# A decoder trunk's side work shifted by half chunks: value-weight sums every third tick, index scores and memory heads one tick later

## The chip, the cores and the metric

The kernel runs on one core of a Trainium2 chip. The metric is the device time of one execution in microseconds (us). Before the change it is 1921.55 us, the median of three runs (1921.13 to 1921.88). A chip core has a matrix engine (TensorE, PE in the profile, with PEld for its weight loads), a vector engine (DVE), an activation engine (ACT), a general engine (GpSimd, POOL) and a sync engine (SP) that issues DMA transfers; DVE, ACT and POOL issue their own instructions in program order, each waiting for the data it reads and for the buffers it writes.

## The reference: two layers of a three-part attention trunk

The input `x` has 512 tokens of width 2048, and there are 256 memory tokens. Two layers are computed, each

```python
h = einsum('bsd,dn->bsn', x, w_in)                 # one projection, split by columns
y_fox = fox_attention(fq, fk, fv, cum_logf) * silu(fg)      # 6 heads, a bias from log-sigmoid forget logits
y_dsa = dsa_attention(rope(dq), rope(dk), dv, rope(iq), rope(ik), iw) * silu(dg)   # 6 heads
y_mem = memory_attention(mq, k_mem, v_mem) * silu(mg)       # 4 heads into the memory tokens
x = layer_norm(ALPHA * x + concat([y_fox, y_dsa, y_mem]) @ w_out)
```

The sparse heads (dsa) keep the 128 best keys of each query. The choice comes from an index score: for each of 16 index heads, `relu(q_idx . k_idx)` times a weight of the query, summed over the heads. The forgetting heads (fox) use a running sum over tokens of `log_sigmoid(f_logit + b_forget)`.

## The kernel before: a stream of weight chunks, with side work hung onto ticks

**The chunks.** All weights pass as chunks of 128 x 2048 float32, in one list that Python writes out in full (the order on every engine is the program's order; nothing reorders it). Each half of a chunk (128 x 1024, a *half chunk*) is loaded by SP into one of 7 `raw` buffers (`load_w`, L259), split into a high and a low part by ACT (`whi`, L218) and DVE (`wlo`, L219) three half chunks ahead of use, and multiplied. Float32 accuracy is made of three matmuls for each product (L225 high x high, L226, L227, the two crossed ones). Sums go into eight PSUM banks that are handed out in turn.

**The stages of a layer.** Key and value of the memory (`mv`, `mk`); the small columns (index key, index weights, forget logits: `small`); eight chunks of index queries (`iq`); then the *values*: 70 chunks of kind `vs` that compute values, gates and other columns for five pairs of column blocks by a seven-product scheme (`PRODUCTS`: P1, P7, Q6, Q4, P2 in a first round of five pairs, and Q5, Q3 in a second round); then the heads' query and key chunks (`fq`, `fk`, `dq`, `dk`), in whose shadow the attention heads run; and the output projection by the same scheme.

**Weight sums.** Some of the seven products multiply a *sum* of weight blocks. Some are made in SBUF: `grow_w` (L284) lets POOL start a DMA that adds a second block onto a `raw` tile in place, and `pair_w` adds on DVE. The others are made in DRAM: POOL starts a DMA that copies one block to a DRAM tile `sum` (L427) and later a second one that accumulates the other block onto it (L407); when the product comes up, SP loads `sum` like any chunk, once the accumulation has landed. In the values stage these are T3 (for P7, all five pairs) and, last of all, T1 of pair 0 (for Q5, two chunks, at the start of the second round). POOL also starts the stores of the values (`store_v`, L980) to DRAM.

**Ticks.** Side work is written as Python generators. `tick()` steps every active generator; it is called after the first half of each chunk and at its end. A generator's `yield n` lets it sit out until the n-th tick from there. Generators begun with `whole=True` sit out the half-chunk ticks in the stages `out` and `vs`. Those that matter here:

- `all_sums` runs the weight sums in a fixed order through `paced` (L430): in the values stage one sum DMA for every `steps` ticks, and there a tick is a whole chunk; the other stages have numbers of their own in the table at L437.
- `small_work` (L602) turns the forget logits into their log-sigmoid: an exponential on ACT, then 15 tiny DVE operations of 128 x 24 (L619 to L631), a transpose, a scan, a store.
- `index_parts` (L672) makes from each roped `iq` chunk two operands `iqs` (high part on ACT, low part on DVE, L679). `index_scores` (L683) does one index head for each tick: six matmuls `ix` (L693, L694) from `iqs`, three ReLU on ACT (`rel`), three multiply-adds on DVE (`acc`, L702 for head 0, L704 after). It begins at L1316 after the first `iq` chunk.
- `mem_head` (L522) does one memory head: queries turned and split, scores `sm`, maximum on DVE (L539, L541), exponential on ACT (L544); a tick later the reciprocal of the sums on DVE (L551) and the scaling of the four blocks `pm` on ACT (L554); a tick later the transposes `ptm` on PE (L562) and their split; a tick later the gate; a tick later the product `po`. Four such heads run in each layer, the first across the end of the values and three in the heads' chunks. Beside them `attend` (L733) does the other heads, and after each `dq` or `dk` chunk DVE does `rope` (L578 to L581) on its bank.

Of the kernel before, what the change touches and what calls it, by code (L numbers as in the profile page):

```python
# [177 lines left out]
def kernel(  # L178
# [248 lines left out]
                            nc.gpsimd.dma_start(sums[key], src)  # L427
                        yield

    def paced(gen, steps=4):  # L430

        n = 0
        for _ in gen:
            n += 1
            while now[1] == "kv":
                yield 1
            yield {"heads": 1, "out": 3, "index": 1 + n % 2}.get(now[1], steps)  # L437
# [84 lines left out]
    def mem_head(l, j):  # L522
        load_head(("mq", j), MEMQ, j)
        km = slot("kmem", F32R)
        nc.sync.dma_start(km.bitcast(F32), km_d[l][j])
        yield 3
        tp = turned(("mq", j), "qk")
        q = slot("qh", F32R), slot("ql", F32R)
        split(tp, *q)
        yield 1  # L530
        k2 = (km[:, 0:256], km[:, 256:512])
        ps = [bank("sm"), bank("sm")]
        for qb in range(4):
            product(ps[qb // 2][:, (qb % 2) * 256:(qb % 2 + 1) * 256],
                    tuple(a[:, qb * P:(qb + 1) * P] for a in q), k2, True, True)
        nm, sums, rec = small("nm", 4), small("sums", 4), small("rec", 4)
        pr = [slot("pm"), slot("pm")]
        for b in range(2):
            nc.vector.tensor_reduce(nm[:, 2 * b:2 * b + 2], ps[b].rearrange("p (a k) -> p a k", a=2),  # L539
                                    axis=AX.X, op=ALU.max, negate=True)  # L540
        nc.vector.tensor_scalar(nm, nm, SCALE, None, op0=ALU.mult)  # L541
        for qb in range(4):
            cols = slice((qb % 2) * 256, (qb % 2 + 1) * 256)
            nc.scalar.activation(pr[qb // 2][:, cols], ps[qb // 2][:, cols], AF.Exp,  # L544
                                 bias=nm[:, qb:qb + 1], scale=SCALE, accum_out=sums[:, qb:qb + 1])
        del km, k2, q
        vm = slot("vmem", F32R)
        nc.sync.dma_start(vm.bitcast(F32), vm_d[l][j])
        load_head(("mg", j), MEMQ + 1, j)
        yield 1  # L550
        nc.vector.reciprocal(rec, sums)  # L551
        for qb in range(4):
            cols = slice((qb % 2) * 256, (qb % 2 + 1) * 256)
            nc.scalar.activation(pr[qb // 2][:, cols], pr[qb // 2][:, cols], AF.Copy,  # L554
                                 scale=rec[:, qb:qb + 1])
        yield 1
        pt = []
        for m in range(2):
            tp = bank("ptm")
            for qb in range(4):  # L560
                c = (qb % 2) * 256 + m * P
                nc.tensor.transpose(tp[:, qb * P:(qb + 1) * P], pr[qb // 2][:, c:c + P], ident)  # L562
            hi, lo = slot("pth", F32R), slot("ptl", F32R)
            split(tp, hi, lo)
            pt.append((hi, lo))
        del pr
        yield 1
        gate(("m", j), turned(("mg", j), "gt"))
        yield 1
        po = bank("po")  # L570
        for m in range(2):
            c = 2 * m * HD
            product(po, (vm[:, c:c + HD], vm[:, c + HD:c + 2 * HD]), pt[m], m == 0, m == 1)
        heads_out(H_FOX + H_DSA + j, ("m", j), po)
# [27 lines left out]
    def small_work(l, sm):  # L602

        yield 1
        tp = bank("iwt")
        for qb in range(4):
            nc.tensor.transpose(tp[:, qb * P:(qb + 1) * P], sm[:, qb * P:(qb + 1) * P], ident)
        tq = tp.rearrange("p (a b) -> p a b", a=4)
        iw = small("iw", 64, bufs=2)
        nc.scalar.activation(iw.rearrange("p (a b) -> p a b", a=4), tq[:, :, 64:80], AF.Copy,  # L610
                             scale=IDX_HEADS ** -0.5)
        idx["w"] = iw
        w = 4 * H_FOX
        x, e, d, s, s2, q = (small(c, w, bufs=2) for c in ("lx", "le", "ld", "ls", "lt", "lq"))
        nc.vector.tensor_copy(x.rearrange("p (a b) -> p a b", a=4), tq[:, :, 96:96 + H_FOX])
        nc.vector.scalar_tensor_tensor(e, x, -1.0, x, op0=ALU.mult, op1=ALU.min)
        nc.scalar.activation(e, e, AF.Exp)
        yield 1
        nc.vector.tensor_scalar(d, e, 2.0, None, op0=ALU.add)  # L619
        nc.vector.reciprocal(d, d)  # L620

        nc.vector.tensor_tensor(s, e, d, op=ALU.mult)
        nc.vector.tensor_tensor(s2, s, s, op=ALU.mult)
        nc.vector.tensor_scalar(q, s2, 1.0 / 17, None, op0=ALU.mult)
        for n in (15, 13, 11, 9, 7, 5, 3):
            nc.vector.scalar_tensor_tensor(q, q, 1.0 / n, s2, op0=ALU.add, op1=ALU.mult)
            if n == 11:
                yield 1
        nc.vector.scalar_tensor_tensor(q, q, 1.0, s, op0=ALU.add, op1=ALU.mult)
        nc.vector.tensor_scalar(x, x, 0.0, None, op0=ALU.min)  # L630
        nc.vector.scalar_tensor_tensor(q, q, -2.0, x, op0=ALU.mult, op1=ALU.add)  # L631
        yield 2
        tp = bank("lft")
        for qb in range(4):
            nc.tensor.transpose(tp[:H_FOX, qb * P:(qb + 1) * P],
                                q[:, qb * H_FOX:(qb + 1) * H_FOX], ident)
        r = slice(0, H_FOX)
        ones, crow = slot("ones"), slot("crow")
        nc.gpsimd.memset(ones[r], 1.0)
        nc.vector.tensor_tensor_scan(crow[r], ones[r], tp[r], 0.0, op0=ALU.mult, op1=ALU.add)  # L640
        nc.gpsimd.dma_start(crow_d[l], crow[r])
        yield 3
        tp = bank("cqt")
        for qb in range(4):
            nc.tensor.transpose(tp[:, qb * H_FOX:(qb + 1) * H_FOX],
                                crow[r, qb * P:(qb + 1) * P], ident[r, r])
        cq = small("cq", w, bufs=2)
        nc.scalar.activation(cq, tp[:, :w], AF.Copy, scale=1 / SCALE)
        forget["cq"] = cq
# [517 lines left out]
    for i, (kind, l, j, col, _) in enumerate(chunks):  # L1167
# [104 lines left out]
        if kind == "mk":  # L1272
            t = slot("kmem", F32R)
            split(ps[:, :256], t[:, 0:256], t[:, 256:512])
            begin(keep((km_d[l][j], t)), 1)
            if j == 3:
                load_index_tables()
        elif kind == "mv" and col == 3:
            for m in range(2):
                hi, lo = slot("vh", F32R), slot("vl", F32R)  # L1280
                split(out_ps[m], hi, lo)
                for part, t in enumerate((hi, lo)):
                    keep_values(l, m, part, t)
        elif kind in ("fq", "fk"):
            hi, lo = slot("qh", F32R), slot("ql", F32R)
            split(ps, hi, lo)
            (ks if kind == "fk" else qs)[kind[0], j] = (hi, lo)
        elif kind in ("dq", "dk"):
            t = rope(ps, cos_d, sin_d, HALVES, P, "rope")
            hi, lo = slot("qh", F32R), slot("ql", F32R)  # L1290
            split(t, hi, lo)
            (ks if kind == "dk" else qs)["d", j] = (hi, lo)
        elif kind == "vs":
            if col == 1:
                val_out(name, pair, zs)
                if name in VAL_ENDS:
                    del chains[VAL_CHAIN[name], pair], zs
        elif kind == "small":
            sm = slot("sm")
            nc.scalar.activation(sm, ps, AF.Copy)  # L1300
            r = slice(96, 96 + H_FOX)
            nc.scalar.activation(sm[r], ps[r], AF.Identity, bias=bfc[r, l:l + 1])
            t = index_rope(ps, 64, 0, nc.vector)
            kh2, kl2 = slot("kh2", F32R), slot("kl2", F32R)
            for r in (0, 64):
                nc.scalar.activation(kh2[r:r + 64], t[:64], AF.Copy)
                nc.vector.tensor_tensor(kl2[r:r + 64], t[:64], kh2.bitcast(F32)[:64],
                                        op=ALU.subtract)
            idx["k"] = (kh2, kl2)
            begin(small_work(l, sm))  # L1310
        elif kind == "iq":
            t = index_rope(ps, P, P, nc.gpsimd)

            begin(index_parts(j, t), 1)
            if j == 0:
                begin(index_scores(l), 2, last=True, whole=True)  # L1316
                begin(first_operands(), last=True)
            if j == 7:
                begin(val_operands(), 3, last=True)
            if j == 7:  # L1320
                index_tabs.clear()
# [147 lines left out]
```

## Time and profile before

| | |
|---|---|
| Median of three runs | 1921.55 us (1921.13 to 1921.88) |
| The profiled execution | 1921.65 us, of which the span from first to last instruction is 1919.9 us |
| Granted TensorE clock, mean | 0.996 of full speed |
| Busy: PE, DVE, ACT, POOL | 1891.7 us (99%), 1482.1 us (77%), 1019.6 us (53%), 364.5 us (19%) |
| DMA, mean rate over the span | 259 GB/s moved (page, part 2) |

PE is busy nearly all the time, so the rows to look for are those with PE's idle time and its releaser, written `[idle us <-releaser]` behind an instruction or as `PE tile line <- engine tile line: total us, times, longest us` in the view of waits. A tile's name in a row stands without its number. `PEclk` is the clock that TensorE was granted in a stretch, and a matmul's listed duration covers its passage through the array, so one follows another at a shorter distance than its duration.

### The profile page before, as it was taken

To read this page: it belongs to the slowest core of one execution; us is meant where nothing else is said; L and a number is where in the kernel's file an instruction comes from. 1 tells how busy PE (TensorE), PEld (TensorE's weight loads), DVE (VectorE), ACT (ScalarE), POOL (GpSimd) and SP (SyncE) were. 2 spreads that over 40 slices of the span, in tenths; PEclk is the share of its full clock that TensorE was granted. 3 is DMA by queue.
4 is the path that set the end of the run, shared out by engine and by line. 5 is a ranking of instruction groups with operands and counts; after the bars stand their busy time and mean duration, and the time that the engine had idled before them with its cause. 6 is when DMAs were issued, how large, how long until landed. Compare 5 with 4: busy or idle time off the path is not lost.

```text
span 1919.9 us, 26427 instructions
## 1 busy us (share of the span) xinstructions
PE 1891.7 (99%) x9250; PEld 1611.7 (84%) x9250; DVE 1482.1 (77%) x2395; ACT 1019.6 (53%) x1598; POOL 364.5 (19%) x603
## 2 busy tenths in 40 slices
PE   9999999999999999999999999999999999999997
PEld 8998888877888888888898988888888888888886
DVE  6889777879745677688897897889987457667898
ACT  5675444444455645555476764444545555555553
POOL 0122122111222011210061221111112121112101
PEclk9999999999999999999999999999999999999999
DMA  9877898889979689898888898887999787889965
GB/s 352 294 214 206 261 245 248 252 211 365 351 230 259 194 245 251 251 355 287 270 239 284 230 236 244 252 241 233 278 321 342 234 214 214 246 248 270 350 203 142
DMA packets 170610, 497.26 MB, mean 259 GB/s; under 512 B 17120, under 2 KB 62176, under 8 KB 162156
## 3 DMA queue, kind: packets, MB, share of 16 engines
q1 hardware_dynamic: 134604, 299.43, 45.3%
q0 software_dynamic: 35872, 196.13, 40.3%
q8 instruction: 73, 1.20, 0.2%
q14 instruction: 61, 0.50, 0.1%
HBM read 448.28 MB, written 166.75 MB: 320 GB/s over the span
## 4 chain that ended last, share of the span: by engine, by line
PE 82%; DVE 7%; ACT 5%; DMA 3%; issue 2%; POOL 0%; SPq 0%; DVEq 0%; ACTq 0%; POOLq 0%
PE v L227 13%; PE v L225 13%; PE v L226 13%; PE c L225 7%; PE c L227 7%; PE c L226 7%; PE z L226 4%; PE z L227 4%; PE z L225 4%; DVE wlo L219 2%; ACT whi L218 2%; DMA raw<-sum 1%; DMA raw<-in_wall_dram 1%; PE ix L693 1%; PE pt L777 1%
## 5 line engine op out<-in xcount | busy, mean ns | idle before, releaser
L219 DVE TENSOR_TENSOR wlo<-raw,whi 128x1024 fp32r<-128x1024 f32 (+1 forms) x521 | 637.7, 1228 | 238.3 <-ACT whi L218 236.0
L218 ACT ACTIVATE whi<-raw 128x1024 fp32r<-128x1024 f32 (+1 forms) x521 | 548.8, 1055 | 427.4 <-PE v L227 276.8
L225 PE MATMUL c<-xh,whi 128*128 128x512 f32 (+1 forms) x800 | 302.0, 377 | 2.9 <-DVE rope L580 2.9
L227 PE MATMUL c<-xh,wlo 128*128 128x512 f32 (+1 forms) x800 | 298.7, 373 | 0.0
L226 PE MATMUL c<-xl,whi 128*128 128x512 f32 (+1 forms) x800 | 298.0, 373 | 0.0
L225 PE MATMUL v<-whi,vxh 128*128 128x512 f32 x640 | 250.8, 392 | 2.8 <-ACT whi L218 1.8
L226 PE MATMUL v<-wlo,vxh 128*128 128x512 f32 x640 | 250.6, 392 | 0.8 <-DVE wlo L219 0.8
L227 PE MATMUL v<-whi,vxl 128*128 128x512 f32 x640 | 250.4, 391 | 0.0
L225 PE MATMUL v<-whi,xh 128*128 128x512 f32 x480 | 186.9, 389 | 0.0
L227 PE MATMUL v<-whi,xl 128*128 128x512 f32 x480 | 186.9, 389 | 0.0
L226 PE MATMUL v<-wlo,xh 128*128 128x512 f32 x480 | 186.9, 389 | 0.0
L226 PE MATMUL z<-wlo,yh 128*128 128x512 f32 (+1 forms) x434 | 168.4, 388 | 2.7 <-DVE wlo L219 2.6
L225 PEld LDWEIGHTS c<-xh,whi 128*128 128x128 f32 x800 | 150.4, 188 | 23.8 <-DVE rope L580 3.5
L225 PE MATMUL z<-whi,yh 128*128 128x512 f32 (+1 forms) x434 | 168.6, 388 | 0.0
L227 PEld LDWEIGHTS c<-xh,wlo 128*128 128x128 f32 x800 | 150.2, 188 | 21.8
L227 PE MATMUL z<-whi,yl 128*128 128x512 f32 (+1 forms) x434 | 168.0, 387 | 0.0
L226 PEld LDWEIGHTS c<-xl,whi 128*128 128x128 f32 x800 | 150.5, 188 | 20.6
L398 POOL TENSOR_TENSOR seen<-mark,mhalf 128x1 f32<-128x1 f32 x96 | 25.9, 270 | 651.9 <-DVE mark L397 614.3
L225 PEld LDWEIGHTS v<-whi,vxh 128*128 128x128 f32 x640 | 120.9, 189 | 28.6 <-ACT whi L218 2.2
L226 PEld LDWEIGHTS v<-wlo,vxh 128*128 128x128 f32 x640 | 120.9, 189 | 26.1 <-DVE wlo L219 1.1
L227 PEld LDWEIGHTS v<-whi,vxl 128*128 128x128 f32 x640 | 120.9, 189 | 25.3
L226 PEld LDWEIGHTS v<-wlo,xh 128*128 128x128 f32 x480 | 90.1, 188 | 18.8
(227 smaller groups left out, 3210.4 us busy)
## 6 DMA issues: line engine op xcount, KB each, us to landing
raw<-in_wall_dram SPq DMA_DIRECT2D x330, 512.0 KB, 7.7
sum<-in_wall_dram POOLq DMA_DIRECT2D x56, 1024.0 KB, 10.9
raw<-sum SPq DMA_DIRECT2D x112, 512.0 KB, 7.4
v<-vraw POOLq DMA_DIRECT2D x120, 256.0 KB, 6.9
raw<-in_wall_dram POOLq DMA_DIRECT2D x48, 512.0 KB, 8.0
vraw<-v SPq DMA_DIRECT2D x80, 256.0 KB, 5.9
other<-in_wall_dram SPq DMA_DIRECT2D x64, 256.0 KB, 9.3
x<-z POOLq DMA_DIRECT2D x28, 256.0 KB, 6.2
```

The costliest lines, as they stand in the source:

```text
L218: nc.scalar.activation(hi, src, AF.Copy)
L219: nc.vector.tensor_tensor(lo, src, hi.bitcast(F32), op=ALU.subtract)
L225: nc.tensor.matmul(ps, ah, bh, start=start, stop=False, skip_group_check=more)
L226: nc.tensor.matmul(ps, ah, bl, start=False, stop=False, skip_group_check=more)
L227: nc.tensor.matmul(ps, al, bh, start=False, stop=stop, skip_group_check=more)
L398: nc.gpsimd.tensor_tensor(seen, mark, mhalf, op=ALU.mult)
L693: nc.tensor.matmul(o, st[:, qb * P:(qb + 1) * P], kh2[:, :w], start=True, stop=False)
L777: nc.tensor.transpose(tp[tb][:, toff + (qb - kt) * P:toff + (qb - kt + 1) * P], pr[b][:, off + kt * P:off + (kt + 1) * P], ident)
```

## The change: four places where a step comes later or sooner

The values stage issues a sum DMA every third chunk and no longer every fourth. The index heads begin one tick (half a chunk) later. The small DVE operations of the forget logits wait a tick more after the exponential and are cut into four pieces by three yields, where one yield cut them in two. In each memory head the scaling L554, and all that follows it, comes one tick later; the reciprocal stays where it was, and so now comes a tick ahead of its use. Nothing is computed differently. Lines from L552 on have a number that is higher by one.

```diff
@@ paced, line 430: how many ticks the generator of the weight sums waits between two steps
-    def paced(gen, steps=4):
+    def paced(gen, steps=3):
@@ mem_head, line 549
         yield 1
         nc.vector.reciprocal(rec, sums)
+        yield 1
         for qb in range(4):
             cols = slice((qb % 2) * 256, (qb % 2 + 1) * 256)
             nc.scalar.activation(pr[qb // 2][:, cols], pr[qb // 2][:, cols], AF.Copy,
@@ small_work, line 617
         nc.scalar.activation(e, e, AF.Exp)
-        yield 1
+        yield 2
         nc.vector.tensor_scalar(d, e, 2.0, None, op0=ALU.add)
...
         for n in (15, 13, 11, 9, 7, 5, 3):
             nc.vector.scalar_tensor_tensor(q, q, 1.0 / n, s2, op0=ALU.add, op1=ALU.mult)
-            if n == 11:
+            if n in (13, 9, 5):
                 yield 1
@@ the main loop, line 1316
             if j == 0:
-                begin(index_scores(l), 2, last=True, whole=True)
+                begin(index_scores(l), 3, last=True, whole=True)
```

Three places in the order of instructions show it. The first is POOL at the end of the first round of the values in layer 0: `sum` are the DRAM sums (L407 the accumulating DMA), `raw<-in_wall_dram` the additions onto weight tiles (L284), `v` the stores of values. Before, around the first of the two last sums, T1 of pair 0:

```order
L284 DMA raw_3537<-in_wall_dram 128x1024
L284 DMA raw_3539<-in_wall_dram 128x1024
L407 DMA sum_3404<-in_wall_dram 128x2048
L284 DMA raw_3581<-in_wall_dram 128x1024
L284 DMA raw_3583<-in_wall_dram 128x1024
L980 DMA v_171<-vraw_3838 128x512
L980 DMA v_171<-vraw_3700 128x512
L980 DMA v_171<-vraw_3841 128x512
L980 DMA v_171<-vraw_3702 128x512
L980 DMA v_170<-vraw_3889 128x512
L980 DMA v_170<-vraw_3891 128x512
L407 DMA sum_3575<-in_wall_dram 128x2048
```

In the changed kernel the two last accumulations stand here:

```order
L284 DMA raw_3122<-in_wall_dram 128x1024
L284 DMA raw_3124<-in_wall_dram 128x1024
L284 DMA raw_3166<-in_wall_dram 128x1024
L284 DMA raw_3168<-in_wall_dram 128x1024
L407 DMA sum_3033<-in_wall_dram 128x2048
L407 DMA sum_3160<-in_wall_dram 128x2048
L981 DMA v_169<-vraw_3403 128x512
L981 DMA v_169<-vraw_3286 128x512
L981 DMA v_169<-vraw_3406 128x512
L981 DMA v_169<-vraw_3288 128x512
```

Both accumulations have moved ahead by one pair of column blocks and more: they now follow the four additions of pair 3 and stand ahead of the stores `v_169` of pair 3, where before they stood among and behind those of pair 4 (`v_171`, `v_170`). No sum stands behind them any more in this stage. `sum_3404` and `sum_3575` are renamed to `sum_3033` and `sum_3160`, since numbers follow the order of writing.

The second is DVE before the first index head in layer 0: `ld` to `lx` are the forget logits' operations, `iqs` the index operands, `wlo` the weight split, `vxl` an operand of the values. Before:

```order
L626 SCALAR_TENSOR_TENSOR lq_864<-lq_864,lt_863 128x24 x3
L397 COPY mark_913<-mhalf 128x1
L219 TENSOR_TENSOR wlo_928<-raw_822,whi_927 128x1024
L626 SCALAR_TENSOR_TENSOR lq_864<-lq_864,lt_863 128x24 x4
L629 SCALAR_TENSOR_TENSOR lq_864<-lq_864,ls_862 128x24
L630 TENSOR_SCALAR lx_859<-lx_859 128x24
L631 SCALAR_TENSOR_TENSOR lq_864<-lq_864,lx_859 128x24
L397 COPY mark_962<-mhalf 128x1
L679 TENSOR_TENSOR iqs_968<-rope_896,iqs_968 64x384
L679 TENSOR_TENSOR iqs_971<-rope_896,iqs_971 64x384
L873 TENSOR_TENSOR vxl_920<-vx_470,vxh_919 128x512
L219 TENSOR_TENSOR wlo_976<-raw_923,whi_975 128x1024
```

and now:

```order
L623 TENSOR_TENSOR ls_862<-le_860,ld_861 128x24
L624 TENSOR_TENSOR lt_863<-ls_862 128x24
L625 TENSOR_SCALAR lq_864<-lt_863 128x24
L627 SCALAR_TENSOR_TENSOR lq_864<-lq_864,lt_863 128x24 x2
L397 COPY mark_954<-mhalf 128x1
L680 TENSOR_TENSOR iqs_960<-rope_896,iqs_960 64x384
L680 TENSOR_TENSOR iqs_963<-rope_896,iqs_963 64x384
L874 TENSOR_TENSOR vxl_912<-vx_470,vxh_911 128x512
L219 TENSOR_TENSOR wlo_968<-raw_915,whi_967 128x1024
L592 TENSOR_TENSOR rope_995<-c_914,tab_715 128x384
L593 TENSOR_TENSOR rope_996<-rope_996,tab_717 128x384
L627 SCALAR_TENSOR_TENSOR lq_864<-lq_864,lt_863 128x24 x2
```

Two of the seven L626 steps stand ahead of the first `iqs` since the last weight split, where before the last four with L629 to L631 did; the rest comes later. On PE, the 24 matmuls of one more half chunk of `iq` now stand ahead of the first `ix`.

The third is ACT in the heads' chunks of layer 0, around the last memory head: `pm` L544 is its exponential, L554 its scaling, `pth` L218 splits of turned probabilities (of `ptm` for a memory head, of `pt` for another head), `whi` the weight split, `tanh` a gate, `qh<-rope` the roped queries. Before:

```order
L544 ACTIVATE pm_6056,sums_6054<-sm_6039,nm_6053 128x256 x2
L544 ACTIVATE pm_6057,sums_6054<-sm_6040,nm_6053 128x256 x2
L218 ACTIVATE whi_6076<-raw_5858 128x1024
L496 ACTIVATE tanh_6115<-gt_6110 128x512
L554 ACTIVATE pm_6056<-pm_6056,rec_6055 128x256 x2
L554 ACTIVATE pm_6057<-pm_6057,rec_6055 128x256 x2
L218 ACTIVATE pth_6153<-pt_6140 128x512
L218 ACTIVATE pth_6157<-pt_6141 128x512
L218 ACTIVATE pthl_6161<-pt_6142 128x256
L218 ACTIVATE whi_6164<-raw_6072 128x1024
L218 ACTIVATE qh_6198<-rope_6192 128x512
```

and now (L555 is the scaling):

```order
L544 ACTIVATE pm_6039,sums_6036<-sm_6022,nm_6035 128x256 x2
L218 ACTIVATE whi_6058<-raw_5849 128x1024
L218 ACTIVATE pth_6097<-ptm_6092 128x512
L218 ACTIVATE pth_6106<-ptm_6101 128x512
L218 ACTIVATE pth_6141<-pt_6128 128x512
L218 ACTIVATE pth_6145<-pt_6129 128x512
L218 ACTIVATE pthl_6149<-pt_6130 128x256
L218 ACTIVATE whi_6152<-raw_6054 128x1024
L218 ACTIVATE qh_6186<-rope_6180 128x512
L496 ACTIVATE tanh_6204<-gt_6199 128x512
L555 ACTIVATE pm_6038<-pm_6038,rec_6037 128x256 x2
L555 ACTIVATE pm_6039<-pm_6039,rec_6037 128x256 x2
```

The scaling stood ahead of `pth<-pt` and the next `whi`; it now stands behind that `whi` and the `qh` of the next roped chunk. In its old place stand the two `pth<-ptm` of the memory head before, which was moved by a tick too.

## The prediction, as recorded before the change was run

> **What bounds the kernel now.** I read the page first, then PE's waits, then PE's own timeline at the waits, and last the chain of waits, to see what each hangs on.
>
> ```profile
> PE 1891.7 (99%) x9250; PEld 1611.7 (84%) x9250; DVE 1482.1 (77%) x2395; ACT 1019.6 (53%) x1598; POOL 364.5 (19%) x603
> ```
>
> PE is busy for all but about 28 us of the span (1919.9 - 1891.7). The change neither adds nor removes a matmul, so all it can win is idle time of PE, or a lowered clock. The view of waits says who ends PE's idle time:
>
> ```profile
> PE ix L693 <- DVE iqs L679: 3.8, 2, 2.6
> PE c L225 <- DVE rope L580: 2.9, 2, 1.5
> PE v L225 <- ACT whi L218: 2.2, 2, 1.8
> PE po L227 <- DVE vl L219: 0.9, 2, 0.5
> ```
>
> The two `ix` waits, one for each layer, are the first index head's. The two behind `rope` and the two `vl` are in the heads' chunks of each layer, where a memory head runs. The largest wait on `whi` lies in layer 0, at 430 us, with two others close behind it. Three stretches, from the windows view (us, then busy time by engine, the clock, the DMA share, GB/s):
>
> ```profile
> 150.00:180.00 30.00, 30.00 (x138) 25.05 (x137) 29.00 (x45) 19.20 (x29) 8.09 (x12) 1.00 0.88 210
> 425.00:446.00 21.00, 17.42 (x62) 13.34 (x61) 15.37 (x24) 9.20 (x11) 2.88 (x4) 0.84 0.93 350
> 300.00:330.00 30.00, 30.00 (x134) 24.84 (x133) 22.42 (x33) 13.84 (x15) 8.51 (x14) 1.00 1.00 293
> ```
>
> **Term 1, the last sums: 7.1 us.** On PE's timeline in layer 0:
>
> ```profile
> 428.10 0.39 PE L226 MATMUL v<-wlo,vxh 128*128 128x512 f32 x1
> 428.32 0.39 PE L227 MATMUL v<-whi,vxl 128*128 128x512 f32 x1
> 430.52 0.49 PE L225 MATMUL v<-whi,vxh 128*128 128x512 f32 x1 [1.80 <-ACT whi L218]
> 431.78 0.80 PE L226 MATMUL v<-wlo,vxh 128*128 128x512 f32 x1 [0.77 <-DVE wlo L219]
> ...
> 437.89 0.40 PE L225 MATMUL v<-whi,vxh 128*128 128x512 f32 x1
> ...
> 439.72 0.39 PE L227 MATMUL v<-whi,vxl 128*128 128x512 f32 x1
> 441.12 0.50 PE L225 MATMUL v<-whi,vxh 128*128 128x512 f32 x1 [1.01 <-ACT vraw L968]
> ```
>
> Undisturbed, one such matmul starts 0.225 us behind the last (428.10 to 428.32, 0.227 over many). From start to start, the three waits cost 2.20 - 0.23 = 1.97, 1.26 - 0.23 = 1.03 and 1.40 - 0.23 = 1.17 us. Between the second and 437.89 lie 14 steps in 6.11 us, where 14 x 0.227 = 3.18 us would do: 2.93 us lost to a halved clock (the window shows 0.84). Together 7.1 us. The chain says what is late:
>
> ```profile
> 414.33 11.01 DMA sum<-in_wall_dram
> 425.40 3.90 DMA raw<-sum
> ```
>
> The accumulation of the second T1 sum starts at 414.33 and lands at 425.4; only then may SP load it. SP and POOL show the whole jam:
>
> ```profile
> SPq L259 <- DMA sum<-in_wall_dram: 39.1, 2, 22.3
> SPq L259 <- DVE wlo L219: 539.9, 219, 12.2
> 384.86 0.33 SPq L259 DMA_DIRECT2D raw<-in_wall_dram  x1
> 407.64 18.56 SPq L259 DMA_DIRECT2D raw<-sum  x4
> 328.49 0.86 POOL L284 DMA_DIRECT2D raw<-in_wall_dram  x1 [2.35 <-DVE wlo L219]
> 395.22 1.20 POOL L407 DMA_DIRECT2D sum<-in_wall_dram  x1
> 353.32 1.86 POOL L980 DMA_DIRECT2D v<-vraw  x3 [22.61 <-DVE vraw L957]
> ```
>
> SP issues nothing from 384.86 to 407.64 and again nearly to 425.4, with all later loads queued behind. In the changed order both accumulations follow the fourth L284 of pair 3, which starts at 328.49, and stand ahead of the stores of pair 3, which start at 353.32. So they are issued in this time, and even if the second only starts at 353 and the two land one behind the other at 12 us each (the median of sums there is in the next fence), both are down by 377, ahead of SP's turn. The earlier L427 copies move ahead likewise. SP then issues its loads when a `raw` buffer comes free, the next bound, and PE's lead of some three half chunks holds, as in 150 to 180 above where PE is busy for 30.00 of 30 us. Layer 1's sums are nearly done when its values begin and its trace has no such wait (SP's row counts two, both here): nothing there. I take all 7.1; the low end of this term is 0 (another wait just as long), the high end 7.1.
>
> What the cover costs: the denser sums lie beside additions onto weight tiles, on one POOL queue. Of these, the first row is undisturbed (155 to 265 us), the second stands behind an accumulation at 396 to 400:
>
> ```profile
> raw<-in_wall_dram POOLq DMA_DIRECT2D x8, 512.0 KB, 6.8
> sum<-in_wall_dram POOLq DMA_DIRECT2D x3, 1024.0 KB, 12.2
> raw<-in_wall_dram POOLq DMA_DIRECT2D x2, 512.0 KB, 13.8
> ```
>
> So an accumulation ahead doubles an addition's landing time from 6.8 to 13.8 us, and PE did not wait then (no wait in its timeline until 428.3). In the new order this meeting comes in pair 2, once. I price it at nothing, since it is the meeting that the trace already shows without a wait.
>
> [...]
>
> **Term 2, the index heads: 4.1 us.** PE and DVE before the first `ix`, layer 0, and PE in layer 1:
>
> ```profile
> 81.28 0.33 PE L226 MATMUL c<-xl,whi 128*128 128x384 f32 x1
> 81.45 0.34 PE L227 MATMUL c<-xh,wlo 128*128 128x384 f32 x1
> 82.98 0.39 PE L693 MATMUL ix<-kh,iqs 128*128 128x256 f32 x1 [1.19 <-DVE iqs L679]
> 80.92 0.83 DVE L626 SCALAR_TENSOR_TENSOR lq<-lq,lt 128x24 f32<-128x24 f32 x4
> 82.37 1.14 DVE L679 TENSOR_TENSOR iqs<-rope,iqs 64x384 fp32r<-64x384 f32 x2
> 1039.89 0.36 PE L693 MATMUL ix<-kh,iqs 128*128 128x256 f32 x1 [2.60 <-DVE iqs L679]
> ```
>
> In layer 0 the gap is 1.53 - 0.17 (the step at this width, 81.28 to 81.45) = 1.36 us, 0.17 over the listed wait; in layer 1 by the same 2.77. DVE runs four tiny steps, then L629 to L631, and only then `iqs`. The half-chunk delay puts 24 matmuls x 0.173 = 4.2 us of PE work between, more than either gap, and `iqs` itself moves ahead of seven tiny operations. The next heads find their operands half a chunk older than before. Gain 4.1; low end 0.
>
> Its price: the 16 heads take one tick each, so with a start half a chunk later one more of them ends up in the values stage, four for three. A head in that stage is three multiply-adds on DVE, which is 29.00 of 30 us busy there:
>
> ```profile
> 155.84 1.67 DVE L704 SCALAR_TENSOR_TENSOR acc<-rel,iw,acc 128x256 f32<-128x256 f32 x3
> ```
>
> DVE has 1.00 us to spare there and gets 1.67 more to do: it falls 0.7 us further behind. It splits three half chunks ahead of PE, each 2.72 us of PE (12 x 0.227), so a lag of 0.7 us is hidden unless the lead is already used up; priced at nothing, at most 0.7 in each layer.
>
> **Term 3, the memory heads: 4.9 us.** In layer 0:
>
> ```profile
> 639.97 0.63 ACT L218 ACTIVATE qh<-rope 128x512 fp32r<-128x512 f32 x1 [0.72 <-DVE rope L581]
> 642.63 0.50 PE L225 MATMUL po<-pth,vh 128*128 128x512 f32 x1 [0.15 <-ACT vh L218]
> 643.84 0.50 PE L227 MATMUL po<-pth,vl 128*128 128x512 f32 x1 [0.47 <-DVE vl L219]
> 650.93 1.71 ACT L554 ACTIVATE pm<-pm,rec 128x256 f32<-128x256 f32 x4 [2.27 <-DVE rec L551]
> 656.35 0.33 PE L227 MATMUL s<-qh,ql 128*128 128x384 f32 x1
> 658.13 0.50 PE L225 MATMUL c<-xh,whi 128*128 128x512 f32 x1 [1.45 <-DVE rope L580]
> ```
>
> The last wait costs 1.78 - 0.17 = 1.61 us, the two before it 0.15 + 0.47 and about 0.17 each to refill: 0.96. So 2.57 in layer 0; layer 1's waits are as long by the totals (`rope` 2.9 for two, `vl` 0.9 for two), less the `vh` one: 2.3. Cause: ACT stands for 2.27 us until the reciprocal comes, then scales for 1.71 us, and the splits behind it hold up DVE's `rope`, whose bank PE wants back. With the tick between, the reciprocal is long done when L555 comes to its turn; ACT scales behind the next `qh`, and the two `pth<-ptm` that take its old place need about 1.3 us (two of the size of that `qh`, 0.63), not 2.27 + 1.71. That is up to 2.7 us earlier for `pth<-pt`, against 1.61 of wait. Also the banks are handed out in turn and a tick's shift puts another bank under that `c`, one that was free longer. Late next is `ptm`, which now waits for a scaling that is issued only half a chunk (5.4 us) ahead, behind `rope` and `qh`. That `qh` ends at 640.6 here; without 1.71 us of scaling ahead it would end at 638.9, the scaling behind it at 640.6, and `ptm`, which now stands right ahead of the `po` of 642.63, is due some 1 us before that `po`, at 641.6. So about 1 us is to spare. I take 4.9; the low end is 0, where as much waiting comes up at `ptm` or `po`.
>
> **The sum.** 7.1 + 4.1 + 4.9 = 16.1 us. Against the profiled execution's 1921.65, which lies 0.1 above the median: 1905.5 us.
>
> **The rivals.**
> 1. *The memory heads only move their wait* to `ptm` or `po`. For it: the narrow 1 us, and that ACT and DVE take turns there. Against: less ACT time ahead of the bank's release. Terms 1 and 2 stay: 1921.65 - 11.2 = 1910.4.
> 2. *DVE falls behind in the first values* by the additional index head: 0.7 us a layer by the spare time above, up to a whole head, 1.67. Then 1906.9 to 1908.8.
> 3. *The first index head still waits*, its place having moved with something DVE does at the later tick: 1909.6. Against: `iqs` comes before that tick on DVE.
> 4. *The jam at 425 stays*, held by the `raw` buffers and not by the sum: 1912.6. For it: SP's waits are mostly for buffers, 539.9 us behind `wlo`. Against: the chain names the sum. If only the slow clock stays, 1908.4.
> 5. *Slower: the denser sums hold up the additions of pairs 1 to 3 in layer 0.* An addition is used some 14 us after its issue at the earliest in the row of 13.8 us without a wait; PE's lead of three splits adds about 4. So it decides beyond about 18 us of landing time. With two sums ahead, 6.8 + 2 x 12.2 = 31 us, a wait of 13 us; in two pairs 26 us, less the 16.1: about 1931. Against: the order puts no two sums between the additions of one pair ahead of it, only in pair 3 behind them. [...]
> 6. *Nothing is gained*, the waits all reappear: 1921.6.
>
> **How the numbers follow.** Forecast 0.52; rival 1 0.16; rival 2 0.10; rival 3 0.05; rival 4 0.07; rival 5 0.05; rival 6 0.05. The likeliest time is 1905.5. The range goes down to 1903.0, 2.5 us for the other waits of PE (on `wlo`, on `whi`) that may move by chance, and up to 1913.0, past rivals 1 to 4; left out are 5 and 6, mixtures of 1 with 4, and a tenth of the forecast's own case, about 0.18. A measurement of this kernel tells about 0.2% from no change, 3.8 us. Faster than 1917.7 are the forecast and rivals 1 to 4: 0.90, less 0.01 for mixtures. Within: rival 6 and half of a milder 5, 0.07. Slower: 0.04.
>
> **What would show it.** Step 1: no wait of SP on `sum<-in_wall_dram` in the values of layer 0, PEclk 1.00 around 425 and PE busy throughout. Step 2: no row `ix <- iqs`, and PE still busy for all of 150 to 180. Step 3: no `c <- rope` and no `po <- vl`; ACT's rows of `pm` on `rec` (2.27 us here) gone; a new row on `ptm` would be rival 1. A wait of `whi` on `raw<-in_wall_dram` between 200 and 400 us would be rival 5.

## The result and the profile after

| | Before | Changed |
|---|---|---|
| Median of four runs | 1921.34 us (1918.55 to 1921.88) | 1904.21 us (1903.45 to 1905.99) |
| Ratio, with 95% interval | | 0.9915 (0.9901 to 0.993) |
| Profiled execution, its span | 1921.65 us, 1919.9 us | 1903.59 us, 1901.8 us |
| Granted clock, mean | 0.996 | 0.998 |

The forecast was 1905.5 us, in a range of 1903.0 to 1913.0. The time lies 1.3 us below it.

PE's waits in the changed kernel (the view of waits; total us, times, longest), all rows of it:

```profile
PE z L226 <- DVE wlo L219: 2.5, 4, 0.7
PE warm L368 <- POOL mhalf L370: 1.4, 1, 1.4
PE v L225 <- ACT memh L218: 0.6, 2, 0.3
PE s L225 <- DVE rec L551: 0.4, 2, 0.2
PE c L227 <- DVE wlo L219: 0.4, 1, 0.4
```

The rows on `iqs`, `rope`, `vl` and `vraw` and the row of `v` on `whi` are gone. One row is new and small: `s` on `rec`, 0.4 us in both layers together. Most of what is left lies at the start and in the output stages, which the change does not touch. The stretches that the prediction named (the windows view: us, busy time by engine, clock, DMA share, GB/s):

```profile
75.00:90.00 15.00, 15.00 (x89) 14.91 (x88) 13.24 (x31) 11.49 (x19) 5.62 (x8) 1.00 0.84 284
150.00:180.00 30.00, 30.00 (x139) 25.07 (x139) 28.90 (x45) 18.73 (x30) 9.05 (x11) 1.00 0.90 208
425.00:446.00 21.00, 21.00 (x94) 17.42 (x93) 18.86 (x26) 10.76 (x14) 3.51 (x4) 1.00 1.01 350
636.00:664.00 28.00, 28.00 (x148) 23.92 (x147) 20.59 (x42) 15.06 (x32) 2.71 (x6) 1.00 0.81 219
1586.00:1613.00 27.00, 27.00 (x145) 23.15 (x144) 20.05 (x42) 14.46 (x31) 3.23 (x7) 1.00 0.78 195
```

PE is busy throughout in all of them, at full clock. Between 425 and 446 us it starts 94 matmuls where it started 62; from 636 to 664 us 148 for 136, by the same row of the kernel before:

```profile
636.00:664.00 28.00, 25.92 (x136) 21.46 (x136) 21.05 (x40) 14.44 (x33) 2.34 (x6) 1.00 0.71 223
```

The span of the profiled execution is 18.1 us shorter, and the three places of the prediction held 16.1 of that. Of the remaining 2 us, 1.1 lie in the first 20 us (PE busy for 16.81 us of them before, 17.88 now), which the change does not reach; in the profiles of the kernels below it runs from 16.5 to 18.0 us, with no order by kernel. The rest is not settled.

The jam on the sums is gone as worked out, in POOL's and SP's own rows (the timeline):

```profile
326.52 0.86 POOL L284 DMA_DIRECT2D raw<-in_wall_dram  x1 [2.35 <-DVE wlo L219]
327.06 2.04 POOL L407 DMA_DIRECT2D sum<-in_wall_dram  x2
...
385.61 19.41 SPq L259 DMA_DIRECT2D raw<-sum  x4
410.08 9.26 SPq L259 DMA_DIRECT2D raw<-in_wall_dram  x5
```

Both accumulations are issued at 327 us, right behind the addition of 326.52. SP issues its first load of a T1 sum at 385.61, where it was 407.64, and no wait of SP on `sum<-in_wall_dram` is left in its view of waits: what spaces its loads now is mostly the release of `raw` buffers (46.3 us of waits on `wlo` from 360 to 440 us), as foreseen. The DMA view of two short stretches shows what the sums meet (median us from issue to landing last; 263 to 273 us, the additions of pair 2 with accumulations among them, then 327 to 329 us, the last two sums):

```profile
raw<-in_wall_dram POOLq DMA_DIRECT2D x4, 512.0 KB, 9.8
...
sum<-in_wall_dram POOLq DMA_DIRECT2D x2, 1024.0 KB, 14.0
```

The last two sums landed after 14.0 us in the median of the two, so both within some 28 us of 327: by 356 us at the latest, about 30 us before SP's turn, and the meeting in pair 2 brought no wait of PE.

### The profile page after: what moved, and what is told of

It reads as the page before. It is cut to its first block, busy times and chain, and to the rows that moved or that the text cites. A ratio compares the mean times of both kernels' runs of the same rounds, so it can differ in the third digit from the quotient of the medians.

```text
span 1901.8 us, 26417 instructions
## 1 busy us (share of the span) xinstructions
PE 1886.0 (99%) x9250; PEld 1610.0 (85%) x9250; DVE 1477.7 (78%) x2395; ACT 1018.7 (54%) x1598; POOL 371.4 (20%) x603
## 4 chain that ended last, share of the span: by engine, by line
PE 89%; DVE 5%; ACT 3%; issue 2%; DMA 1%; POOL 1%; SPq 0%; DVEq 0%; ACTq 0%; POOLq 0%
PE v L227 14%; PE v L225 14%; PE v L226 14%; PE c L227 9%; PE c L225 9%; PE c L226 9%; PE z L226 4%; PE z L227 4%; PE z L225 4%; PE pt L778 1%; DVE wlo L219 1%; PE ix L694 1%; PE ix L695 1%; PE po L227 1%; PE po L226 1%
## 5 line engine op out<-in xcount | busy, mean ns | idle before, releaser
L218 ACT ACTIVATE whi<-raw 128x1024 fp32r<-128x1024 f32 (+1 forms) x521 | 548.5, 1055 | 420.4 <-PE v L227 273.8
```

What stands on the lines that cost most here:

```text
L218: nc.scalar.activation(hi, src, AF.Copy)
```

## The experiments: each part alone, each part left out, and the limits

All kernels of the table were timed in four or more runs beside the kernel before. A saving "by the ratio" is (1 - ratio) x 1921.3 us, and a difference between two kernels the difference of their ratios times 1921.3; an interval of a ratio is about 2.5 us to either side, so a difference of two ratios is uncertain by some 3.5 us.

| Kernel | Median, us | Ratio to before (95%) |
|---|---|---|
| the change | 1904.21 | 0.9915 (0.9901 to 0.993) |
| sums alone | 1912.11 | 0.9958 (0.9946 to 0.9971) |
| index and logits alone | 1918.91 | 0.9992 (0.9983 to 1.0001) |
| memory heads alone | 1915.04 | 0.9972 (0.9961 to 0.9983) |
| change without the sums | 1912.71 | 0.995 (0.9937 to 0.9963) |
| change without index and logits | 1908.5 | 0.9934 (0.9922 to 0.9947) |
| change without the memory heads | 1909.89 | 0.994 (0.9927 to 0.9954) |
| change, index start set back | 1906.01 | 0.9921 (0.9909 to 0.9934) |
| change, logits set back | 1905.27 | 0.992 (0.9907 to 0.9932) |
| change, reciprocal late too | 1905.21 | 0.992 (0.9906 to 0.9934) |
| change, a sum every 2 chunks | 1905.11 | 0.991 (0.9896 to 0.9923) |
| change, a sum every chunk | 1915.46 | 0.9966 (0.9952 to 0.9979) |

### The three parts, alone and left out

The sums alone, on the kernel before:

```diff
-    def paced(gen, steps=4):
+    def paced(gen, steps=3):
```

> The kernel before with the sums every third chunk and nothing else. By the theory of the terms: the 7.1 us around 428 to 441 us go (or 7.2 to 4.2, where the kernel before runs without its slow clock), the waits on iqs (4.1) and in the memory heads (5) stay: about 1914.3 us. By the rival (the last wait is for raw buffers, the sum only comes last by chance) another wait of some us stands at 428: above 1917.

Measured: 8.1 us less by the ratio. No wait is left between 420 and 450 us, and the waits on `rope` and `vl` stand as before, those on `iqs` with 2.5 us in all for 3.8:

```profile
420.00:450.00 30.00, 30.00 (x134) 24.82 (x134) 26.74 (x38) 15.17 (x18) 4.60 (x6) 1.00 0.96 319
```

The other way round, the change with `steps=4`:

> The changed kernel with the sums every fourth chunk again, so the index and memory-head edits without the sums. By the prediction's term: 7.1 us more, 1911.3. By the measurement of the sums alone on the kernel before (9.1 us): 1913.3. The wait on the last two sums should stand again at 425 to 441 us; where the clock stays at 1.00 there, the wait on vraw at its end should be longer (2.6 us) than where it is halved (1.0 us), since a slow PE lets ACT catch up.

Measured: 6.7 us more by the ratio (8.5 by the medians), and the jam is back. The clock stayed at full until its last wait (PE's steps are 0.23 us ahead of it, 0.43 behind it), and that wait, on `vraw`, is 2.64 us, as expected for this case. The term of 7.1 us holds from both sides, and so does its cause: nothing but the distance of the sums differs.

The memory heads alone (the one `yield 1` behind the reciprocal added to the kernel before) and the change without it:

> The kernel before with the scaling of the memory heads a tick after the reciprocal. By the theory 4.9 to 5.4 us go in the heads' chunks of both layers: about 1916.3. By the rival that the waits only move: 1920 to 1921.5.

> The changed kernel with the scaling of the memory heads back beside the reciprocal. By the prediction's term: 4.9 us more, 1909.1, with the waits on rope, vl and vh in both layers as before. By the measurement of this edit alone (6.1 us): 1910.3.

Measured: 5.4 us less alone, 4.8 us more when left out, by the ratios. In the change without it PE's view of waits has the old rows back, and no others of their size in the heads' chunks:

```profile
PE c L225 <- DVE rope L580: 2.9, 2, 1.5
PE po L227 <- DVE vl L219: 0.9, 2, 0.5
```

The index heads with the logits alone (`begin(index_scores(l), 3, ...)`, `yield 2` behind the exponential, yields at 13, 9 and 5), and the change without these:

> The kernel before with the index heads a tick later and the logits' small operations in four pieces. By the theory: both gaps before the first ix go, 4.1 us, and the jam at 428 stays: about 1917.3. By the rival (the additional index head in the values makes DVE late) 1.4 to 3.4 us come back between 150 and 200 us and in the same place of layer 1: 1918.7 or more.

> The changed kernel without the two edits on the index and the logits: sums and memory heads alone. By the term of the prediction the two gaps of 1.4 and 2.8 us stand again: 1908.3. By the measurement of these two edits on the kernel before (2.3 us): 1906.5. If they do nothing for the time: 1904.2.

Left out of the change, they cost 3.7 us by the ratio (4.3 by the medians), near the term of 4.1; in the profile the waits on `iqs` that are back come to 2.5 us in all. Alone on the kernel before they save 1.5 us by the ratio, with an interval from 3.3 us saved to 0.2 us lost, which the 4.1 us lie outside of. Its profile has no wait on `iqs` and no new one between 150 and 200 us, so the rival that the additional head makes DVE late falls. What it has is a jam at 428 us of larger size than in the profile of before, and in that kernel the jam is still there to vary. Between these two profiles the jam's size makes 0.9 us of the difference (below). PE's waits on `z`, in the output stages, are 1.8 us longer in its profile as well; why is not settled.

### What of the index edits is needed

The index start back to 2 with the logits in four pieces; and the start at 3 with the logits as before:

> The changed kernel with the index heads' start set back a tick, the logits' operations still in four pieces. DVE then has some 0.8 us less ahead of the first iqs than in the kernel before (two tiny steps and L629 to L631). If the tick is what removes the wait: gaps of about 0.55 us (layer 0) and 1.95 us (layer 1) at the first ix stand again, 2.5 us in all, 1906.7. If the cut of the logits' operations does it alone: no gap, 1904.2.

> The changed kernel with the logits' operations in two pieces as before, the index heads still a tick late. If the tick removes the wait: no gap at the first ix in either layer, 1904.2. If the cut is needed too: a gap of 1 us or more in layer 1, 1905.5 or more.

With only the logits' edit of the two, a wait at the first `ix` remains in layer 0 (first row, PE's timeline); with neither edit it is that of before in layer 0 (second row) and 1.36 us in layer 1 (third row):

```profile
82.88 0.39 PE L694 MATMUL ix<-kh,iqs 128*128 128x256 f32 x1 [0.17 <-DVE iqs L680]
```

```profile
83.33 0.39 PE L694 MATMUL ix<-kh,iqs 128*128 128x256 f32 x1 [1.18 <-DVE iqs L680]
1028.87 0.36 PE L694 MATMUL ix<-kh,iqs 128*128 128x256 f32 x1 [1.36 <-DVE iqs L680]
```

With only the tick no row of `ix` on `iqs` is in the view at all. So either edit removes most of this wait: 0.5 us of it is left in both layers with the logits' cut alone (its row reads `0.5, 2, 0.4`), none with the tick alone. The times, 1906.0 and 1905.3 us, are not told apart from the change's by their intervals. The forecast of 2.5 us left for the cut alone was too high, in good part because it started from a layer-1 gap of 2.77 us that turned out to be one execution's. In another execution of the kernel before, the row was

```profile
1041.61 0.35 PE L693 MATMUL ix<-kh,iqs 128*128 128x256 f32 x1 [1.71 <-DVE iqs L679]
```

### Is it the early reciprocal or the late scaling?

In the prediction the memory heads' waits came from ACT, which stood up to 2.27 us for the reciprocal ahead of the scaling. To tell that from the mere shift of all later steps by a tick, the reciprocal was put a tick late too, directly ahead of the scaling:

```diff
-        yield 1
+        yield 2
         nc.vector.reciprocal(rec, sums)
-        yield 1
         for qb in range(4):
```

> The changed kernel with the reciprocal a tick later too, directly ahead of the scaling, so that everything behind it stays a tick late as in the changed kernel but ACT waits for the reciprocal again. If the late place of the scaling and of what follows (other PSUM banks, the scaling behind qh) is what removes PE's waits: none come back, 1904.2. If it is the early reciprocal: PE waits for rope, vh or vl or for ptm in both layers, up to the 5 us of before, 1906 to 1909.

ACT's group for the scaling (the lines view: busy us, mean ns, idle before and its releaser) in the kernel before, in the change, and in this kernel:

```profile
L554 ACT ACTIVATE pm<-pm,rec 128x256 f32<-128x256 f32 x32 | 13.7, 498 | 13.4 <-DVE rec L551 13.4
```

```profile
L555 ACT ACTIVATE pm<-pm,rec 128x256 f32<-128x256 f32 x32 | 13.6, 496 | 0.0
```

```profile
L554 ACT ACTIVATE pm<-pm,rec 128x256 f32<-128x256 f32 x32 | 13.7, 498 | 8.0 <-DVE rec L551 8.0
```

ACT's wait is back with 8.0 of 13.4 us; at the last memory head of layer 0 it is 1.08 us, where it was 2.27. PE's waits on `rope`, `vl` and `vh` are not back: none is among its rows, and the time is 1905.2 us, 1.0 above the change by either measure, inside the intervals. So in the late place PE's waits stay away though ACT stands for the reciprocal again, and the early reciprocal adds too little to be told from noise. A full wait of 2.27 us in the late place was not run.

How the late place helps can be read on DVE. In the kernel before, DVE stands for ACT's `pth` ahead of the `rope` that PE waits for (first row); in this kernel (second row) and in the change the same step has no wait, for the scaling no longer stands ahead of that `pth` on ACT:

```profile
653.15 1.29 DVE L219 TENSOR_TENSOR ptl<-pt,pth 128x512 fp32r<-128x512 f32 x2 [2.32 <-ACT pth L218]
```

```profile
641.51 1.28 DVE L219 TENSOR_TENSOR ptl<-pt,pth 128x512 fp32r<-128x512 f32 x2
```

This speaks for the order on ACT; what the other bank under the next `c` adds was not taken apart.

### How dense the sums may be

The change with the sums every second chunk, and at every chunk:

> The changed kernel with a sum every second chunk. If the distance of the sums only has to be short enough for the last two to be down before SP's turn: 1904.2, no PE wait between 150 and 450 us. If denser sums cost (rival 5, additions landing beyond 18 us): waits of whi on raw there and a time above 1906.

> The changed kernel with a sum at every chunk. The order has one accumulation between the additions of pairs 0 and 2 each, so by the trace so far additions of 12 to 14 us and no PE wait: 1904.2. By rival 5: two sums ahead of an addition, landing at 25 us or more, a wait of some 7 us or more in one or two pairs: 1911 to 1918.

Every second chunk is as good as every third, and no better: there was no more wait to remove. At every chunk the time is 9.8 us above the change by the ratios, within what rival 5 gave. PE's timeline and ACT's in this kernel:

```profile
225.68 0.50 PE L225 MATMUL v<-whi,vxh 128*128 128x512 f32 x1 [1.03 <-ACT whi L218]
226.94 0.79 PE L226 MATMUL v<-wlo,vxh 128*128 128x512 f32 x1 [0.76 <-DVE wlo L219]
246.00 0.49 PE L225 MATMUL v<-whi,vxh 128*128 128x512 f32 x1 [2.32 <-ACT whi L218]
...
224.57 1.06 ACT L218 ACTIVATE whi<-raw 128x1024 fp32r<-128x1024 f32 x1 [3.06 <-DMA raw<-sum]
244.89 1.06 ACT L218 ACTIVATE whi<-raw 128x1024 fp32r<-128x1024 f32 x1 [7.51 <-DMA raw<-in_wall_dram]
```

And the DMA view: POOL's issues from 200 to 245 us with a sum every chunk, and SP's from 190 to 245 us, in this kernel and then in the change:

```profile
sum<-in_wall_dram POOLq DMA_DIRECT2D x3, 1024.0 KB, 19.9
raw<-in_wall_dram POOLq DMA_DIRECT2D x4, 512.0 KB, 20.1
...
raw<-in_wall_dram SPq DMA_DIRECT2D x7, 512.0 KB, 12.6
raw<-sum SPq DMA_DIRECT2D x4, 512.0 KB, 15.7
```

```profile
raw<-in_wall_dram SPq DMA_DIRECT2D x8, 512.0 KB, 5.0
raw<-sum SPq DMA_DIRECT2D x4, 512.0 KB, 8.3
```

The additions onto weight tiles land after 20.1 us, and ACT, then PE at 246.00, waits for them (the addition issued at 224.34 us, the `whi` behind it at 244.89). With a sum every second chunk the additions of the same stretch took 11.5 us, and PE was busy for all of 190 to 250 us. This is the mechanism of rival 5 with its threshold between: no wait at 13.8 us, waits at 20.1.

The late landing is not all of it. That addition was also issued late, by POOL's timeline in this kernel:

```profile
216.47 0.88 POOL L284 DMA_DIRECT2D raw<-in_wall_dram  x1 [2.29 <-DVE wlo L219]
223.80 0.83 POOL L407 DMA_DIRECT2D sum<-in_wall_dram  x1 [6.46 <-DMA sum<-in_wall_dram]
224.34 1.20 POOL L284 DMA_DIRECT2D raw<-in_wall_dram  x1
```

POOL stands 6.46 us at an accumulation until a sum's DMA has landed, by the order the copy that it adds onto, and the addition behind it in POOL's order waits with it. From the second to the third addition of the pair it takes 7.9 us here and 2.7 in the change (211.80 to 214.52), where POOL has no such wait from 150 to 250 us; nor has it with a sum every second chunk. The copy and the accumulation of one sum are too close together when a sum DMA is issued for each chunk of 5.4 us and a sum lands after 19.9. How much of the 9.8 us is the late issue and how much the slow landing was not taken apart.

The PE wait at 225.68 is on one of SP's loads of a sum, on another queue. With the denser sums SP's loads of weights take 12.6 us here for 5.0 in the change, and its loads of sums 15.7 for 8.3, so the loads slow down with a queue that they do not stand in. How the DMA engines share their time between the queues is not shown.

### The kernel before once more

> The kernel before once more, for its clock at 425 to 446 us. Where the slow clock goes with the wait: clock 0.84 and 17.4 of 21 us busy there again, 1921.5. [...]

1924.82 us in its one run, and the clock was lowered there again (0.89 from 420 to 450 us). The time is 3.3 us above the one expected for that, and above all runs of this kernel beside it (1918.62 to 1923.25). Most of that lies in the first 20 us, where the clock was lowered too:

```profile
0.00:20.00 20.00, 16.86 (x59) 12.73 (x60) 9.81 (x13) 11.12 (x15) 0.74 (x7) 0.91 0.90 307
```

PE starts 59 matmuls there where it started 68 in the first execution, at clock 1.00: 9 x 0.227 = 2.0 us. An execution with clock 1.00 at the jam was not among the profiles of this kernel. What this and the other kernels that still have the jam show is put together below.

## Why the prediction was right, point by point

- **PE's idle time is all there is to win, in three places.** Right: the waits named are gone, no others of their size came, and the three parts, alone, save 8.1, 5.4 and 1.5 us, left out, cost 6.7, 4.8 and 3.7, where 7.1, 4.9 and 4.1 were reckoned. Either three add up to about 15 us, of the 16.3 that the change's own ratio gives. Each part is uncertain by 2 to 3.5 us, so that the sum of 16.1 came within 0.2 us of the measured saving is in part luck.
- **Term 1, the sums.** Right in mechanism and size: the accumulations are issued at 327 us, right behind the fourth addition of pair 3, at the early end of the stretch that the order gave (328 to 353 by the times of before). They land some 30 us before SP needs them, and SP now stands for buffers, without a wait of PE. Wrong in the split of its 7.1 us: 2.93 us were charged to the lowered clock. A run of the jam at full clock (the last section) shows that a part of it would have been waiting instead.
- **Its cover, priced at nothing.** Right: additions among accumulations in pair 2 landed after 9.8 us (median of four) without a wait of PE.
- **Term 2, the index heads.** The tick covers the wait in both layers, as worked out, and the additional head in the values costs nothing: PE is busy for 30.00 of 30 us from 150 to 180. The size was one execution's for layer 1 (2.77 us; the wait was 2.60 there, and 1.71 in another execution). Four other profiles with the old start and the logits as before list 2.5 to 2.9 us for both layers where this one listed 3.8; with 0.17 us for each gap that makes 2.8 to 3.2, so 4.1 us was about 1 us too much.
- **Term 3, the memory heads.** Right in size (4.8 to 5.4 for 4.9), and `ptm` has no wait, so the spare time of about 1 us sufficed. Of the causes that it named, the reciprocal's wait on ACT proved the lesser. With 8.0 of its 13.4 us back, PE waits for `rope` or `vl` no more than in the change. The place of the scaling behind the next `qh` carries the gain; the share of the other banks, also named, is not known.
- **The rivals.** Rivals 1 to 4 did not come: no `ptm` or `po` wait, no lateness of DVE, no `ix` wait, no wait of PE for want of `raw` buffers at 425. Rival 5 was real, but its point of decision lies between a sum every second chunk and one every chunk, and a part of it is POOL's own standing for a copy, which the prediction did not name.

## What to carry to other kernels

Where one queue issues work for others in a fixed order, read the chain back from the late load to the instruction that started it, and issue that instruction earlier, where its queue has time to spare. It can be too dense: a sum DMA for each 5.4 us chunk was too many here, where sums then landed after 19.9 us and an accumulation stood for its own copy. An engine's own idle time (ACT's 13.4 us on the reciprocal) is no measure of what its removal gives; ask which instruction of the bounding engine waits, and test the shift without the cure. A gap read in one execution can be that execution's: the largest of the index gaps was 0.9 us shorter in the next.

## What the runs showed of the hardware

The cost of the lowered clock was not what its rows suggest. The jam at 420 to 450 us (windows view) in the kernel before, in its second execution, with the memory heads alone, with index and logits alone, and in the change, which has no jam, in this order, each from its own kernel:

```profile
420.00:450.00 30.00, 26.42 (x102) 20.81 (x101) 20.49 (x29) 11.09 (x14) 2.88 (x4) 0.89 0.89 299
```

```profile
420.00:450.00 30.00, 26.11 (x99) 20.38 (x98) 21.27 (x33) 11.12 (x14) 2.88 (x4) 0.89 0.90 296
```

```profile
420.00:450.00 30.00, 25.11 (x108) 19.55 (x107) 20.89 (x30) 12.02 (x15) 2.88 (x4) 1.00 0.92 314
```

```profile
420.00:450.00 30.00, 24.61 (x98) 19.03 (x97) 19.97 (x29) 11.05 (x13) 2.88 (x4) 0.94 0.89 311
```

```profile
420.00:450.00 30.00, 30.00 (x134) 24.85 (x133) 26.69 (x39) 15.01 (x17) 4.59 (x6) 1.00 1.00 322
```

At 30 / 134 = 0.224 us each, the first four lose 32, 35, 26 and 36 matmuls, or 7.2, 7.8, 5.8 and 8.1 us. With the clock at 1.00 all through, 5.8 us are lost, so the lowered clock costs some 1.4 to 2.3 us and not 2.93. This is an estimate, from single executions of different kernels. The wait at the end of the jam shows where the rest is, in the kernel before (timeline, clock lowered ahead of it) and with the memory heads alone (clock full):

```profile
441.12 0.50 PE L225 MATMUL v<-whi,vxh 128*128 128x512 f32 x1 [1.01 <-ACT vraw L968]
```

```profile
439.88 0.50 PE L225 MATMUL v<-whi,vxh 128*128 128x512 f32 x1 [2.63 <-ACT vraw L969]
```

At full clock PE came to this place earlier and stood longer for ACT. In the second execution of the kernel before the clock was lowered too, and that wait was 2.22 us, so the exchange is not the same each time. With index and logits alone there was no such exchange: the clock fell only behind the last wait, and 8 steps from 439.13 us took 3.44 us where 1.82 would do, 1.6 us that no later wait of the jam gave back. The same holds for the change without the sums, whose jam loses 36 matmuls too:

```profile
420.00:450.00 30.00, 24.79 (x98) 19.15 (x98) 20.53 (x30) 11.12 (x13) 2.89 (x4) 0.94 0.92 319
```

Whether the clock falls there is also not the same each time: after first waits of 0.6 to 1.8 us it fell at 431 us in the kernel before (0.51 from 431 to 438 us), only behind the last wait with index and logits alone (the row below: 0.85 from 439 us on, after a wait of 2.63 us that ended at 439.13), and not at all with the memory heads alone, whose last wait was 2.63 us too.

```profile
439.00:450.00 11.00, 10.87 (x41) 8.87 (x42) 9.35 (x12) 4.43 (x6) 1.78 (x2) 0.85 1.06 350
```

What makes the clock fall is not shown. It stayed at 1.00 behind the wait of 2.60 us on `iqs` in layer 1 of the kernel before (windows view, 1039 to 1045 us) and behind the 2.63 us with the memory heads alone, and it fell behind 2.63 us with index and logits alone and behind 2.64 us in the change without the sums. No row of PE's waits here is longer.
